# A token mixer with a chunked delta-rule recurrence: the recurrence's products as full 128x128 matmuls, k and r projected together

## The chip, the core and the metric

One core of a Trainium2 chip runs the whole step in one launch. Five engines work side by side, each through its own queue in order: TensorE (PE) multiplies matrices into PSUM, VectorE (DVE), ScalarE (ACT) and GpSimd (POOL) compute, SyncE (SP) issues transfers. The metric is the time of one execution on the device in microseconds, lower is better.

## What is computed

One layer on 2048 prompt tokens and on 8 sequences of 8 sample tokens, width 1024, all in float32. A convolution branch of 512 columns and a recurrent branch of 8 heads of 64 read the same normalised input, and an output projection joins them.

```python
xn = rms_norm(x, norm_g)
p = xn @ w_in                                # 1024 x 4224
# convolution branch: four groups of 512 columns
u = cg * h
z = conv_w[0]*u_ext[:, 0:T] + conv_w[1]*u_ext[:, 1:T+1] + conv_w[2]*u_ext[:, 2:T+2]
y_conv = bg * z * silu(gc)
# recurrent branch: r, k, v, two low-rank inputs (wl, al) and a gate, mixed with the previous token
pr = pr + mu_shift * (pr_prev - pr)
decay = exp(-DECAY_SCALE * sigmoid(w0 + tanh(wl) @ w_dec2))
a = sigmoid(a0 + al @ w_a2)
# per token and head, S is 64 x 64
sa = S @ (-kk_t)
S = S * w_t + sa (kk_t * a_t)^T + v_t k_t^T
o_t = S @ r_t
# group norm of o per head, bonus, gate; then
y = concat(y_conv, y_rwkv) @ w_out;  return rms_norm(x + y), states
```

## The kernel before, in words

Tokens stand along the free axis, features on the partitions. The prompt is done in two halves of 1024 tokens (`hf`), each in three blocks (`half_blocks`, line 79): 256, 384 and 384 tokens, in chunks of 64; the sample tokens ride with block 0 of the first half as one more chunk. The 8 heads are 4 pairs; one pair fills 128 partitions, head 0 above head 1. The main loop (line 915) makes 8 steps, one for each half and pair.

A projection (`project`, line 297) multiplies one or two tiles of 128 columns of `w_in` with a block: 24 matmuls for a tile and block, since inputs and weights are each split into a high and a low part of type float32r (three products, 8 slices of the 1024 rows). `load_w` (line 288) loads a tile's weights in two pieces and splits them on ACT and POOL; there are two buffers each for the high and the low part.

A step does, in program order:

- `rwkv_pair` (line 415). Tile k for all blocks, then tile r for all blocks, into two long tiles of the `hp` buffers (four of them); then v and the gate g in turn, and between them the front of each block. `after_k` makes the decays, their running products W, the scaled vectors `L` (first 64 columns from k, last 64 from r) and `bk`; `after_r` calls `amat`, which multiplies `bk` with `L` for each chunk and head, and masks the product into `AB` (solve matrix and output matrix) and into the other half of `L`; `store_blocks` sends the diagonal 32x32 blocks of `AB` out; `after_v` makes the bonus.
- `inverse` (line 625). Loads these blocks (`na`) and solves 32 columns by forward substitution on DVE (`subst`, two DVE instructions a row), sends the result round through DRAM into `AB`, and makes the off-diagonal blocks with 32x32 matmuls, with ACT and DVE reading one PSUM tile in turn (lines 671, 672).
- `wkv` (line 711), the recurrence. `group_tiles` transposes `bk` and v of up to four chunks. Then each `chunk` (line 714): L with state and v, the copy `xs`, AB with `xs`, the scaling `u` (line 736), `bt` with u, and the new state by two DVE instructions (line 740) that also read `tS`, the decayed old state (ACT). Each matmul is done once for each head, on 64 of the 128 rows or columns; an f32 matmul runs as two passes. Outputs add up in `oo`, one tile for a block, and `gn_out` normalises and stores them.
- `conv_group` (line 317), one of the four groups of the convolution branch: four single projections, h, C, B and G. At step 3 it comes before the next half's `xprep` and the inverse.

The framework orders the instructions when it builds: each engine takes what comes first in the program among what its own timing model has ready. So the projections of `conv_group` and of the next pair stand between the recurrence's matmuls in PE's queue. `T(pool, shape, tag, bufs)` is a tile out of `bufs` buffers. All waits are made by the framework; accesses of two engines to one PSUM tile are put in turn. PSUM has eight banks: `pj` 2 (projections), `ax` 2 (fronts), `cx` 1 (transposes, inverse), `ca`, `cb`, `oo` 1 each (recurrence).

The last part (`out_tile`, line 882) multiplies 17 tiles of up to 128 tokens with `w_out`, 48 matmuls of 512 columns each.

Of the kernel before, what the change touches and what calls it, by code (L numbers as in the profile page):

```python
# [10 lines left out]
BF16 = mybir.dt.bfloat16  # L11
# [25 lines left out]
C_MASK, C_SMASK, C_SCM, C_SCS, C_BM = 0, 128, 256, 640, 704  # L37
NMASK = 712
# [5 lines left out]
def constants():  # L44
# [11 lines left out]
    m[:, C_MASK:C_MASK + 64] = strict  # L56
    m[:, C_MASK + 64:C_MASK + 128] = incl
    m[:, C_SMASK:C_SMASK + 64] = strict & same
    m[:, C_SMASK + 64:C_SMASK + 128] = incl & same
# [28 lines left out]
def trunk_kernel(ctx, tc, I, O):  # L88
# [24 lines left out]
    def tmp():  # L113
        return T("tmp", [128, TW], "t", 7)
# [12 lines left out]

    def mm(out, lhsT, rhs, start=True, stop=True):
        pe.matmul(out, lhsT=lhsT, rhs=rhs, start=start, stop=stop)  # L129
# [3 lines left out]
    # constants and parameters  # L133
# [22 lines left out]
    def load_masks():  # L156
        for q in range(2):
            m = slice(q * NMASK // 2, (q + 1) * NMASK // 2)
            t = tmp()[:, :NMASK // 2]
            act.dma_start(out=t, in_=I["masks"][:, m])  # L160
            pool.tensor_copy(out=msk[:, m], in_=t)
# [26 lines left out]
    def rsqrt(x, n, rows=128, tag="x"):  # L188
        """x <- 1/sqrt(x) on [rows, n] of positive floats."""
# [14 lines left out]
    # normalised inputs, transposed and split  # L204
# [4 lines left out]
    def xprep(hf):  # L209
# [8 lines left out]
        def staging():  # L218
            stage[0] += 1
            if stage[0] % 6 == 5:  # L220
                return T("half", [128, HALF + SAMP], "la1", 1)[:, :D]
            if stage[0] % 6 == 0 and hf == 0:
                return T("pair", [128, 32, 32], "na", 1).rearrange("p a b -> p (a b)")
            return T("half", [128, 1108], "hp", 4)[:, :D]
# [63 lines left out]
    def load_w(src):  # L288
        wh = T("w", [128, KT, 128], "wh", 2, F32R)
        wl = T("w", [128, KT, 128], "wl", 2, F32R)  # L290
        for q in range(2):
# [24 lines left out]
    # convolution branch  # L316
    def conv_group(xs, hf, g):
        sp = 80 if hf == 0 else 0
        u = T("half", [128, 1108], "hp", 4)
        z = T("half", [128, 1108], "hp", 4)  # L320
        us = u[:, 0:80].rearrange("p (b j) -> p b j", j=10)
        up = u[:, sp:sp + 2 + HALF]

        def ev_h(bl, ps):
            if bl.samp:
                copy(us[:, :, 2:10], s9(ps)[:, :, 1:9])
                copy(us[:, :, 0:2], stc[:, g, :].rearrange("p (b j) -> p b j", j=2))
            if bl.i == 0:
                copy(up[:, 0:2], ucarry[:, g, :])
            copy(up[:, 2 + bl.p0:2 + bl.p0 + bl.np], ps[:, bl.c0:bl.cols])  # L330

        def ev_c(bl, ps):
            if bl.samp:
                mul(us[:, :, 2:10], us[:, :, 2:10], s9(ps)[:, :, 1:9])
                for b in range(1):
                    zs = s8(z)
                    copy(zs, us[:, :, 0:8], scale=pcol(P_CW, g))
                    stt(zs, us[:, :, 1:9], pcol(P_CW, 4 + g), zs, ALU.mult, ALU.add)
                    stt(zs, us[:, :, 2:10], pcol(P_CW, 8 + g), zs, ALU.mult, ALU.add)
# [3 lines left out]
            a, n = bl.p0, bl.np  # L343
            cur = up[:, 2 + a:2 + a + n]
            mul(cur, cur, ps[:, bl.c0:bl.cols])
            zp = z[:, bl.o:bl.o + n]
            copy(zp, up[:, a:a + n], scale=pcol(P_CW, g))
            for j in (1, 2):
                t = tmp()[:, 0:n]
                copy(t, up[:, a + j:a + j + n], scale=pcol(P_CW, 4 * j + g))  # L350
                pool.tensor_tensor(out=zp, in0=zp, in1=t, op=ALU.add)
            if bl.i == 2:
                copy(ucarry[:, g, :], up[:, HALF:HALF + 2])
                if hf == 1:
                    act.dma_start(out=O["conv_p"][:, g, :], in_=ucarry[:, g, :])
# [17 lines left out]

        yield from project(xs, hf, (g * 128, ev_h))
        yield from project(xs, hf, (2 * CW + g * 128, ev_c))
        yield from project(xs, hf, (CW + g * 128, ev_b))
        yield from project(xs, hf, (3 * CW + g * 128, ev_g))

    # token shift
    def shifter(hf, i, dst):  # L380
        state = {}

# [628 lines left out]
```

## Time and profile before

| | |
|---|---|
| median of 3 runs | 1671.4 us (1671.36 to 1675.69) |
| span of the profiled execution | 1669.8 us |
| instructions | 29362 |
| PE busy | 1548.2 us, 93% |
| DVE busy | 1046.6 us, 63% |
| ACT busy | 652.7 us, 39% |
| POOL busy | 338.2 us, 20% |
| projections and output, PE matmuls (`pj`) | 5568 |

Busy times come from one profiled execution. Matmuls are pipelined: one's time from start to end is longer than the distance to the next one's start, so the distance of starts tells what a matmul costs PE. The granted clock is 1.00 at full speed (2.4 GHz) and 0.5 at the lower level (1.2 GHz); the share given for a stretch is a mean.

### The profile page before, as it was taken

What the parts mean: (1) busy time and instruction counts of PE and PEld (TensorE: products, weight loads), DVE (VectorE), ACT (ScalarE), POOL (GpSimd) and SP (SyncE); (2) the same over time, 40 slices, a digit from 0 to 9 for tenths busy, and PEclk for the clock granted to TensorE, in tenths of its full rate; (3) what the DMA queues carried; (4) which work ended last, traced back from release to release, by engine and by line L of the source; (5) the groups of instructions that cost most, each with busy time, mean ns of one, the idle gap of its engine ahead of it and who ended that gap; (6) DMA issues with size and microseconds to landing.
All of it is one profiled execution on the core that took longest, in us unless ns stands there. A gap on an engine that the chain in (4) does not pass through costs nothing.

```text
span 1669.8 us, 29362 instructions
## 1 busy us (share of the span) xinstructions
PE 1548.2 (93%) x11088; PEld 1293.2 (77%) x11088; DVE 1046.6 (63%) x3101; ACT 652.7 (39%) x1657; POOL 338.2 (20%) x395
## 2 busy tenths in 40 slices
PE   4989999989989999879988998899989999899997
PEld 4979778887778778867778778877887788567885
DVE  6377557765776469775577457745774577566554
ACT  5333345324532455254442454245424542342221
POOL 3233112421032103321033112311231123100000
PEclk9989999899989999989989998999899989799999
DMA  5101201120012102331012101210121023523441
GB/s 170 50 28 44 62 30 31 44 67 29 21 47 56 47 23 60 92 96 37 22 34 63 46 23 35 63 46 23 34 63 46 23 59 92 155 77 124 139 145 51
DMA packets 112463, 99.99 MB, mean 60 GB/s; under 512 B 61561, under 2 KB 85625, under 8 KB 112322
## 3 DMA queue, kind: packets, MB, share of 16 engines
q1 hardware_dynamic: 107024, 87.23, 18.0%
q10 hardware_dynamic: 5266, 10.86, 1.8%
q8 instruction: 88, 1.44, 0.4%
q14 instruction: 53, 0.43, 0.1%
q0 software_dynamic: 32, 0.03, 0.0%
HBM read 75.30 MB, written 22.75 MB: 59 GB/s over the span
## 4 chain that ended last, share of the span: by engine, by line
PE 64%; DVE 22%; DMA 5%; issue 4%; ACT 3%; SPq 1%; POOL 1%; POOLq 0%; ACTq 0%; DVEq 0%
PE pj L129 42%; PE ca L129 5%; PE ax L129 5%; DVE sub L123 5%; DVE xi L123 4%; PE cb L129 4%; PE oo L129 2%; DVE hp L123 2%; PE cx L129 2%; DMA na<-dn 2%; DVE bk L123 1%; DVE t L120 1%; PE cx L688 1%; DVE hp L120 1%; PE ax L282 1%
## 5 line engine op out<-in xcount | busy, mean ns | idle before, releaser
L129 PE MATMUL pj<-xh,wh 128*128 128x384 f32 (+3 forms) x1856 | 660.5, 356 | 31.8 <-DVE hp L123 30.4
L129 PE MATMUL pj<-xh,wl 128*128 128x384 f32 (+3 forms) x1856 | 658.8, 355 | 0.0
L129 PE MATMUL pj<-xl,wh 128*128 128x384 f32 (+3 forms) x1856 | 656.3, 354 | 2.6 <-POOL xl L207 2.2
L129 PEld LDWEIGHTS pj<-xh,wh 128*128 128x128 f32 x1856 | 360.3, 194 | 69.4 <-DVE hp L123 28.3
L129 PEld LDWEIGHTS pj<-xl,wh 128*128 128x128 f32 x1856 | 361.1, 195 | 30.2 <-POOL xl L207 3.0
L129 PEld LDWEIGHTS pj<-xh,wl 128*128 128x128 f32 x1856 | 360.2, 194 | 27.2 <-issue 2.7
L207 POOL TENSOR_TENSOR wl<-wr,wh 128x512 fp32r<-128x512 f32 x132 | 173.4, 1328 | 459.0 <-ACT wh L117 321.4
L117 ACT ACTIVATE wh<-wr 128x512 fp32r<-128x512 f32 x132 | 80.2, 625 | 162.9 <-PE pj L129 119.1
L117 ACT ACTIVATE tS<-sv,wc 64x64 f32<-64x64 f32 x256 | 88.0, 344 | 130.2 <-DVE sv L120 104.3
L129 PE MATMUL ax<-L,bk 64*128 64x128 f32 x528 | 89.5, 325 | 35.7 <-DVE bk L123 25.8
L129 PEld LDWEIGHTS ax<-L,bk 64*128 64x128 f32 x528 | 74.0, 219 | 54.2 <-POOL wl L207 26.7
L120 DVE SCALAR_TENSOR_TENSOR sv<-cb,wc,tS 64x64 f32<-64x64 f32 x240 | 67.9, 283 | 63.5 <-PE cb L129 52.2
L123 DVE TENSOR_TENSOR sub<-xi,na 128x126 f32<-128x126 f32 (+22 forms) x248 | 91.1, 367 | 17.3 <-DMA na<-dn 10.0
L117 ACT ACTIVATE t<-pj,prm 128x384 f32<-128x384 f32 (+3 forms) x170 | 68.8, 433 | 62.7 <-PE pj L129 59.5
L516 POOL TENSOR_TENSOR bk<-t,t 64x384 f32<-64x384 f32 (+2 forms) x56 | 56.2, 1003 | 173.8 <-ACT t L488 91.4
L736 DVE TENSOR_SCALAR u<-ca,Q 128x64 f32<-128x64 f32 x128 | 36.2, 283 | 85.7 <-PE ca L129 85.4
L123 DVE TENSOR_TENSOR xi<-xi,sub 128x126 f32<-128x126 f32 (+22 forms) x248 | 83.0, 335 | 7.3
L129 PEld LDWEIGHTS ca<-sv,L 128*64 128x64 f32 x528 | 43.4, 136 | 38.6 <-DVE sv L120 12.2
L726 DVE COPY xs<-ca 128x64 f32<-128x64 f32 x128 | 28.7, 225 | 68.7 <-PE ca L129 58.5
L129 PE MATMUL ca<-sv,L 128*64 128x64 f32 x528 | 68.4, 247 | 0.0
L123 DVE TENSOR_TENSOR AB<-ax,msk 64x384 f32<-64x384 f32 (+2 forms) x88 | 48.6, 553 | 28.9 <-PE ax L129 27.9
L123 DVE TENSOR_TENSOR hp<-pj,hp 128x512 f32<-128x512 f32 (+1 forms) x34 | 23.4, 689 | 62.6 <-PE pj L129 61.7
(201 smaller groups left out, 2027.1 us busy)
## 6 DMA issues: line engine op xcount, KB each, us to landing
wr<-in_w_in SPq DMA_DIRECT2D x132, 256.0 KB, 2.7
hp<-in_x_prompt SPq DMA_DIRECT2D x29, 512.0 KB, 3.7
la<-yd SPq DMA_DIRECT2D x16, 512.0 KB, 3.9
out_y_p<-hp ACTq DMA_DIRECT2D x16, 512.0 KB, 2.7
na<-dn SPq DMA_DIRECT2D x16, 256.0 KB, 4.0
hp<-in_w_out SPq DMA_DIRECT2D x8, 512.0 KB, 4.1
yd<-hp SPq DMA_DIRECT2D x16, 192.0 KB, 1.9
yd<-c SPq DMA_DIRECT2D x16, 192.0 KB, 1.9
```

The costliest lines, as they stand in the source:

```text
L117: act.activation(out=out, in_=in_, func=AF.Copy, scale=scale, bias=bias)
L120: eng.scalar_tensor_tensor(out=out, in0=in0, scalar=scalar, in1=in1, op0=op0, op1=op1)
L123: dve.tensor_tensor(out=out, in0=in0, in1=in1, op=op)
L129: pe.matmul(out, lhsT=lhsT, rhs=rhs, start=start, stop=stop)
L207: eng.tensor_tensor(out=lo, in0=src, in1=hi.bitcast(F32), op=ALU.subtract)
L282: pe.transpose(out=ps[:, k, :], in_=xt[:, kk * 128:(kk + 1) * 128], identity=ident)
L516: pool.tensor_tensor(out=S.bk[bl.i][hs, chs, h, :], in0=ta[hs, a:a + n].rearrange("p (c j) -> p c j", j=64), in1=wi[hs, a:a + n].rearrange ...
L688: pe.transpose(out=pb[:, i, :], in_=S.bk[bi][:, ca + i].rearrange("p a t -> p (a t)"), identity=ident)
L726: dve.tensor_copy(out=xs_, in_=px)
L736: dve.tensor_scalar(out=u, in0=pu, scalar1=S.Q[:, q:q + 1], scalar2=None, op0=ALU.mult)
```

## The change

The recurrence: `bk` is transposed in the front, block by block, into `G` (one 128x128 block for each head and chunk, made of the transposed `bk` in the head's columns and the masked output matrix in the other head's columns). A chunk is then two products of L for 128 columns, one product of both heads' solve (`AB` of this and the next chunk as 128 columns, times a block-diagonal `xd`), and two products of G, which give the state's part and the output's part at once. Outputs are read once for each group of up to four chunks, by an ACT copy and a DVE sum. The first copy and the scaling are each divided between DVE and ACT by heads; `tS` moves to POOL. `L`, `G`, `AB` are made once and kept; `bk` has two buffers for three tiles.

The projections: k and r are projected together, block by block, into tiles of one block (`kr`, three buffers), and `after_kr` runs the block's front right behind them; v with g, h with C and B with G likewise. Weights are loaded in three pieces. The buffers `hp` go from four to two and `t` from seven to four, with tiles of their own for `sq`, `td`, `ta`. The matmuls of `amat` alternate between the heads. The bonus product with v moves to POOL.

```diff
     def load_w(src):
...
-        for q in range(2):
-            wr = T("w", [128, 4, 128], "wr", 2)
-            sync.dma_start(out=wr, in_=src[:, q * 4:q * 4 + 4, :])
-            split(wh[:, q * 4:q * 4 + 4, :], wl[:, q * 4:q * 4 + 4, :], wr, pool)
+        for k in (slice(0, 3), slice(3, 6), slice(6, 8)):
+            raw = T("w", [128, 3, 128], "wr", 2)[:, :k.stop - k.start, :]
+            sync.dma_start(out=raw, in_=src[:, k, :])
+            split(wh[:, k, :], wl[:, k, :], raw, pool)
...
+    LP, GP, ABP = [[], []], [[], []], []
+    for i, mx in enumerate((5, 6, 6)):
+        for h in range(2):
+            LP[h].append(T("pair", [128, mx, 128], f"L{h}{i}"))
+            GP[h].append(T("pair", [128, mx, 128], f"G{h}{i}"))
+        ABP.append(T("pair", [128, mx + 1, 64], f"AB{i}"))
+    XD = [T("pair", [128, 128], f"xd{i}") for i in range(2)]
...
         def amat(bl, ca, n, smask=False):
...
+            pas = [AX([128, n, 128]) for h in range(2)]
+            for i in range(n):
+                for h, hs in heads():
+                    mm(pas[h][:, i, :], bk[hs, ca + i].rearrange("p a t -> p (a t)"), L[h][hs, ca + i, :])
...
             for h, hs in heads():
...
+                mul(AB[hs, cs, :], pas[h][hs, :, hs], m(hs, 0, 64))
+            ab = AB[:, cs, :]
             pool.tensor_tensor(out=ab, in0=ab, in1=S.Q[:, q0:q0 + n].unsqueeze(2).to_broadcast([128, n, 64]), op=ALU.mult)
...
+            pb = CX([128, n, 128])
+            for i in range(n):
+                pe.transpose(out=pb[:, i, :], in_=bk[:, ca + i].rearrange("p a t -> p (a t)"), identity=ident)
+            for h, hs in heads():
+                copy(G[h][:, cs, hs], pb[:, :, hs])
+            for h, hs in heads():
+                mul(L[h][other(h), cs, :], pas[h][other(h)], m(other(h), 64 * h, 128))
+                mul(G[h][hs, cs, other(h)], pas[h][hs, :, other(h)], m(hs, 64, 64))
...
+        yield from project(xs, hf, (CONV_COLS + CW + p * 128, shifter(hf, 4 + p, to_tmp("k"))),
+                           (CONV_COLS + p * 128, shifter(hf, p, to_tmp("r", after_kr))))
+        yield from project(xs, hf, (CONV_COLS + 2 * CW + p * 128,
+                                    shifter(hf, 8 + p, lambda bl: (S.v[bl.i], lambda: after_v(bl)))),
+                           (CONV_COLS + 3 * CW + 128 + p * 128, shifter(hf, 13 + p, to_tmp("g", after_g))))
...
     def chain_banks():
-        return PS([128, 4, 64], "ca", 1), PS([128, 2, 64], "cb", 1)
+        return [PS([128, 2, 4, 64], f"ch{h}", 1) for h in range(2)] + [PS([128, 4, 128], "cu", 1)]
...
             for h, hs in heads():
-                mm(px[hs], L[h][:, c, 0:64], sv[:, i, h, :])
+                mm(pc[h][:, 0, i, :], S.L[h][bi][:, c, :], sv[:, i, h, :])
+            xd = XD[i % 2]
+            if sample is None:
+                tS = T("ch", [128, 64], "tS", 2)
+                for h, hs in heads():
+                    pool.tensor_scalar(out=tS[hs], in0=sv[hs, i, h, :], scalar1=S.wc[hs, wc:wc + 1], scalar2=None,
+                                       op0=ALU.mult)
+                dve.tensor_copy(out=xd[0:64, 0:64], in_=pc[0][0:64, 0, i, :])
+                copy(xd[64:128, 64:128], pc[1][64:128, 0, i, :])
...
+            pu = pc[2][:, i, :]
+            mm(pu, S.AB[bi][:, c:c + 2, :].rearrange("p c t -> p (c t)"), xd)
+            dve.tensor_scalar(out=sv[0:64, i, 0, :], in0=pu[0:64, 0:64], scalar1=S.Q[0:64, q:q + 1], scalar2=None,
+                              op0=ALU.mult)
+            copy(sv[64:128, i, 1, :], pu[0:64, 64:128], scale=S.Q[64:128, q:q + 1])
             for h, hs in heads():
+                mm(pc[h][:, 1, i, :], S.G[h][bi][:, c, :], sv[:, i, h, :])
...
                 for h, hs in heads():
+                    stt(nxt(h)[hs], pc[h][hs, 1, i, :], S.wc[hs, wc:wc + 1], tS[hs], ALU.mult, ALU.add)
...
+            for h, hs in heads():
+                os_ = other(h)
+                o_ = ob[os_, ca:ca + n, :]
+                copy(o_, pc[h][os_, 0, 0:n, :])
+                tt(o_, pc[h][os_, 1, 0:n, :], o_, ALU.add)
```

## Rows read from the trace of the kernel before

**Rows 1.** The page, part 1: busy us, share of span, instructions.

```profile
PE 1548.2 (93%) x11088; PEld 1293.2 (77%) x11088; DVE 1046.6 (63%) x3101; ACT 652.7 (39%) x1657; POOL 338.2 (20%) x395
```

**Rows 2.** The page, part 4: the chain that ended last, by engine.

```profile
PE 64%; DVE 22%; DMA 5%; issue 4%; ACT 3%; SPq 1%; POOL 1%; POOLq 0%; ACTq 0%; DVEq 0%
```

**Rows 3.** Windows: us, busy (instructions) of PE, PEld, DVE, ACT, POOL; PEclk, DMA, GB/s.

```profile
1216.00:1250.00 34.00, 29.76 (x169) 28.95 (x168) 24.88 (x70) 7.36 (x15) 10.92 (x10) 0.90 0.19 56
1250.00:1268.00 18.00, 18.00 (x219) 16.25 (x218) 6.61 (x15) 5.91 (x18) 4.35 (x6) 1.00 0.37 88
1268.00:1330.00 62.00, 62.00 (x562) 45.82 (x562) 30.37 (x125) 28.65 (x86) 5.59 (x6) 1.00 0.07 24
1330.00:1383.00 53.00, 48.77 (x274) 43.77 (x274) 42.37 (x99) 24.36 (x56) 17.05 (x18) 0.87 0.20 56
```

**Rows 4.** Timeline of PE, one chunk: start, us to the last end, what, xcount.

```profile
1301.02 0.34 PE L129 MATMUL pj<-xh,wh 128*128 128x384 f32 x1
1301.29 0.33 PE L129 MATMUL cb<-u,bt 64*64 64x64 f32 x4
...
1301.67 0.45 PE L129 MATMUL pj<-xl,wh 128*128 128x384 f32 x1
1301.95 0.34 PE L129 MATMUL pj<-xh,wl 128*128 128x384 f32 x1
1302.22 0.33 PE L129 MATMUL ca<-sv,L 128*64 128x64 f32 x2
...
1303.03 0.44 PE L129 MATMUL pj<-xh,wh 128*128 128x384 f32 x1
1303.31 0.34 PE L129 MATMUL pj<-xl,wh 128*128 128x384 f32 x1
1303.58 0.33 PE L129 MATMUL ca<-xs,AB 64*64 64x64 f32 x4
1303.84 0.44 PE L129 MATMUL pj<-xh,wl 128*128 128x384 f32 x1
1304.12 0.34 PE L129 MATMUL pj<-xh,wh 128*128 128x384 f32 x1
1304.29 0.33 PE L129 MATMUL pj<-xl,wh 128*128 128x384 f32 x1
```

**Rows 5.** Timeline of PE around six full f32 passes in a front.

```profile
311.20 0.34 PE L129 MATMUL pj<-xl,wh 128*128 128x384 f32 x1
311.38 0.72 PE L129 MATMUL ax<-cst,t 128*128 128x2 f32 x6
311.96 0.42 PE L129 MATMUL pj<-xh,wl 128*128 128x384 f32 x1
312.22 0.34 PE L129 MATMUL pj<-xh,wh 128*128 128x384 f32 x1
```

**Rows 6.** Groups by line: busy us, mean ns of one | idle before <-releasers.

```profile
L129 PE MATMUL ax<-L,bk 64*128 64x128 f32 x528 | 89.5, 325 | 35.7 <-DVE bk L123 25.8 <-DVE nwyg L120 4.0 <-DVE L L123 3.1
L736 DVE TENSOR_SCALAR u<-ca,Q 128x64 f32<-128x64 f32 x128 | 36.2, 283 | 85.7 <-PE ca L129 85.4
L672 DVE COPY na<-cx 32x192 f32<-32x192 f32 (+1 forms) x24 | 8.2, 341 | 20.1 <-ACT na L117 19.8
L117 ACT ACTIVATE tS<-sv,wc 64x64 f32<-64x64 f32 x256 | 88.0, 344 | 130.2 <-DVE sv L120 104.3 <-DVE nwyg L196 8.4 <-DVE gv L841 7.5
L760 POOL COPY sv<-sst 64x64 f32<-64x64 f32 x16 | 3.8, 236 | 32.6 <-PE cb L129 32.1
L207 POOL TENSOR_TENSOR wl<-wr,wh 128x512 fp32r<-128x512 f32 x132 | 173.4, 1328 | 459.0 <-ACT wh L117 321.4 <-PE pj L129 126.5 <-DMA AB<-dx 6.7
L194 DVE TENSOR_SCALAR nwag<-gv 128x6 int32<-128x6 int32 (+2 forms) x24 | 5.6, 235 | 0.4
```

**Rows 7.** Timeline of DVE while POOL multiplies bk.

```profile
1334.31 0.71 DVE L194 TENSOR_SCALAR nwag<-gv 128x6 int32<-128x6 int32 x1
```

**Rows 8.** The page, part 6: DMA issues, KB each, us to landing.

```profile
hp<-in_x_prompt SPq DMA_DIRECT2D x29, 512.0 KB, 3.7
```

More of the change, by code (lines that the diff above doesn't have):

```diff
@@ L126, in mul, with heads, other @@
         tt(out, in0, in1, ALU.mult)
+    def heads():
+        return ((0, slice(0, 64)), (1, slice(64, 128)))
+    def other(h):
+        return slice(64 - 64 * h, 128 - 64 * h)
     def mm(out, lhsT, rhs, start=True, stop=True):
@@ L406, in shifter, with clear_blocks @@
         return ev
+    LP, GP, ABP = [[], []], [[], []], []
[5 more added lines that the diff above has]
+    XD = [T("pair", [128, 128], f"xd{i}") for i in range(2)]
+    def clear_blocks():
+        for i in range(3):
+            pool.memset(ABP[i], 0.0)
+            for h, hs in heads():
+                pool.memset(GP[h][i][other(h), :, other(h)], 0.0)
+        for t in XD:
+            pool.memset(t, 0.0)
     class Pair:
@@ L468, in after_k @@
             decays(bl)
[L469 to L470 removed]
+            sq, td, ta = (T("tmp", [128, TW], n, 1) for n in ("sq", "td", "ta"))
+            cc, cum = sq, td
+            act.activation(out=sq[:, :nt], in_=kb, func=AF.Square, scale=pcol(P_KK, p))
+            pq = AX([128, 4, 2])
+            for j in range(bl.nch // 2):
+                a = (SAMP if bl.samp else 0) + j * 128
+                mm(pq[:, j, :], sq[:, a:a + 128], hsel)
+            if bl.samp:
+                mm(pq[0:64, 3, :], sq[:, 0:64], hsel)
             act.activation(out=td[:, :nt], in_=pd, func=AF.Tanh, scale=0.5, bias=hwa[:, p:p + 1])
@@ L682, in group_tiles @@
     def group_tiles(S, bi, ca, n):
-        bt = T("ch", [128, 4, 128], "bt", 2)
         sv = T("ch", [128, 4, 2, 64], "sv", 2)
-        pb = CX([128, 4, 128])
-        for i in range(n):
-            pe.transpose(out=pb[:, i, :], in_=S.bk[bi][:, ca + i].rearrange("p a t -> p (a t)"), identity=ident)
-        copy(bt[:, 0:n, :], pb[:, 0:n, :])
         o = ca * 64
@@ L722, in chunk @@
             if sample is None:
                 for h, hs in heads():
-                    vs = slice(64, 128) if h == 0 else slice(0, 64)
-                    mm(pm[hs], bt[vs, i, hs], sv[vs, i, h, :], start=True, stop=False)
-                dve.tensor_copy(out=xs_, in_=px)
-                tS = T("ch", [128, 64], "tS", 2)
-                for h, hs in heads():
-                    copy(tS[hs], sv[hs, i, h, :], scale=S.wc[hs, wc:wc + 1])
-            else:
-                tt(xs_, px, sample, ALU.add)
@@ L747, in chunk @@
-            for h, hs in heads():
-                mm(po[hs], AB[hs, c, 64:128], us[h][hs], start=False, stop=True)
+                    stt(nxt(h)[hs], pc[h][hs, 1, i, :], S.wc[hs, wc:wc + 1], tS[hs], ALU.mult, ALU.add)
         groups = []
@@ L801, in sample_chunk @@
         for a in range(2):
-            copy(pts[:, a, :].rearrange("p (b j) -> p b j", j=8), pp_[:, :, a, :])
+            for h, hs in heads():
+                copy(pts[hs, a, :].rearrange("p (b j) -> p b j", j=8), pp_[hs, :, a ^ h, :])
         pt = CX([128, 128])
@@ L805, in sample_chunk @@
         xo = T("ch", [128, 8, 64], "c2", 4)[:, :2]
-        for a in range(2):
-            for h, hs in heads():
-                copy(xo[hs, a, :], pt[a * 64:a * 64 + 64, hs])
-        po = PS([128, 1, 64], "oo", 1)
-        chunk(0, 0, 0, None, bt, sv, 0, po[:, 0], None, chain_banks(), sample=xo[:, 0, :])
-        tt(ob[:, 0, :], po[:, 0], xo[:, 1, :], ALU.add)
+        for h, hs in heads():
+            copy(xo[hs, 0, :], pt[0:64, hs])
+            copy(xo[other(h), 1, :], pt[64:128, hs])
+        pc = chain_banks()
+        chunk(0, 0, 0, None, sv, 0, None, pc, sample=xo[:, 0, :])
+        for h, hs in heads():
+            os_ = other(h)
+            tt(xo[os_, 1, :], pc[h][os_, 0, 0, :], xo[os_, 1, :], ALU.add)
+            tt(ob[os_, 0, :], pc[h][os_, 1, 0, :], xo[os_, 1, :], ALU.add)
         zm = T("ch", [128, 8, 64], "c2", 4)[:, :8]
```

243 lines of the change are left out of this document (93 added, 150 removed).

## The prediction, made before the change was run

> **What bounds the kernel now.** I read the busy shares first [rows 1]: TensorE (PE) is busy 93% of 1669.8 us, VectorE 63%. The reader is to see that only PE comes near the span; the chain that ended last says the same, PE 64% and DVE 22% of it [rows 2]. The time outside the profiled span is the median less the span, 1.6 us (0.1%); I add nothing for it and work against 1669.8.
>
> An average hides four stretches, so next I cut one period of the second half (167 us, one head pair) into windows [rows 3]. 1216 to 1250: the substitution on DVE, PE filled by the convolution's projections, clock 0.90. 1250 to 1268: the rest of the inverse. 1268 to 1330: the recurrence, 16 chunks in 62 us, 3.87 us each; PE is busy every microsecond at full clock, DVE 30 of 62. 1330 to 1383: the next pair's front (decays, L, bk, the masked products): DVE 42 of 53, PE's clock 0.87. So the recurrence is bound by PE, the front by DVE and its hand-overs, and they stand one behind the other.
>
> What PE does in a chunk is in its timeline [rows 4]. From 1301.02 to 1304.29 is one chunk, 3.27 us. Two projection matmuls side by side start 0.17 apart (1304.12, 1304.29); seven of them start in the chunk, 1.19 us. The other **2.08 us** are three groups of small matmuls, 24 passes (an f32 matmul is two). It is not the passes that cost: four 64x64 passes end within 0.33 us, but from the last projection matmul before such a group to it are 0.27 us where 0.17 is usual (1303.31 to 1303.58), and the first one after it keeps the next away 0.28 (1303.84 to 1304.12). Entering and leaving a small group costs about 0.1 each.
>
> **The change, part by part.**
>
> *Chunk on PE.* 24 small passes become 10 full ones: 4 with L, 2 with the pair of AB blocks, 4 with G. The nearest full f32 passes are the six with 2 columns [rows 5]: between 311.20 and 312.22 lie two projection matmuls (0.34) and six passes, so 0.68 us, 0.113 a pass, entering and leaving included. Ten are 1.13. Saved: 0.95 x 132 chunks (the front's 528 passes of L with bk are four a chunk [rows 6]) = **-125 us** of PE. Bounds: 0.08 a pass (four 64x64 passes in 0.33 [rows 4]) gives -169; if enter and leave stay at 0.2 for each of three groups, the saving is 0.35, -46. I take the six full passes; they are the same kind with the same weights' width.
>
> Here a page speaks against the change. The Trainium skill (TensorEngine Tiling (Array Packing), Theoretical Speedup) promises up to 2x where one dimension is at most 64, by cutting the array into tiles, which this edit gives up; the same page (Key Properties) says that changing the tiling mode drains the array. The 0.1 on either side of a group agrees with the second. By the first alone the saving would be nil (rival 4).
>
> *Front on PE.* The 528 passes of L with bk (mean 325 ns [rows 6]) stay, but alternate between the heads' row halves and fill two banks at once. Between 0 and half of their 89.5 us; DVE sets this stretch, so I take -10. Transposes of bk move from the chunk groups into the front, same number; their copies become two for each group instead of one, on ACT.
>
> *Chain of a chunk.* The hand-overs stay five (L, copy, AB, scale, G, update), but three things change. The scale was one DVE instruction, 283 ns [rows 6]; now DVE scales one head and ACT the other out of one PSUM bank. The program makes them take turns: where before both read one bank (line 672) DVE sat 19.8 us over 24 times for ACT [rows 6]. One 64x64 ACT step is 344 ns: +0.34 a chunk. At the end of each group of up to four chunks ACT copies and DVE adds the outputs before the next group may write those banks: two steps of at least 0.28 and 0.34 with hand-overs, about 0.9, five groups a pair, +0.28 a chunk. tS goes from ACT to POOL, beside the matmuls: 236 ns for a 64x64 copy [rows 6], nothing on the path unless POOL's queue is in a weight split of 1.33 us [rows 6]. Shorter PE groups give back 0 to 0.95; I take 0.3.
>
> POOL beside DVE has a price that a row shows: a 6-element DVE step takes 0.71 us while POOL multiplies bk [rows 7]; its mean is 0.24 [rows 6]. The Trainium skill (SBUF — State Buffer, Who interferes with whom) lets a DVE step with one SBUF input outside the two-port modes run free of POOL. If it holds for the chain, whose steps read PSUM, this price is nil; the row is the other bound.
>
> *Front in time.* k and r now come block by block, into three small tiles, with the block's front right behind, and L, G, AB are held per block. Block 0 of the next pair can write its L once the recurrence has passed block 0. So two of three block fronts can lie inside the recurrence, where DVE is idle half the time; only block 2 must follow it: 53 becomes 18 (bounds 18 and 53). Its DVE steps queue with the chain: between 0 and (0.71 - 0.24) x 5 = 2.4 a chunk; I take +0.5, one such wait.
>
> Recurrence: 3.87 + 0.34 + 0.28 - 0.30 + 0.50 = 4.69 a chunk, 75 us. Period: 34 + 18 + 75 + 18 = 145 for 167, -22.
>
> *Weights.* All projections now run in pairs, so both weight buffers are taken until the pair ends; before, single tiles let the next load ahead. A tile's split is 2 x 1.33 us of POOL [rows 6], three pieces instead of two, the same elements. It lies under 24 matmuls of the first tile's block 0, 4.1 us at 384 columns and 2.7 at 256 (by columns). Cover is just short, 0.5 us x 32 pairs: **+15** (0 to 43, one uncovered piece each).
>
> *At nothing:* conv's u per block, the split L copies, bonus product on POOL, clearing the blocks at the start (POOL waits for loads there). Staging and output tiles have 2 buffers for 4: a 512 KB load is 3.7 us [rows 8], an output tile is 48 matmuls of 512 columns, about 11 us, so it stays covered; uncovered, 17 x 3.7 = +63.
>
> **Two sums.** By PE work: 1669.8 - 125 - 10 + 15 = 1550, all of today's idle time and slow clock kept. By stretches: six periods with a successor in the same half, 6 x -22 = -132; the last pair runs beside the output projection, where PE is the bound, 17 x -0.95 = -16; +15: 1537. I forecast **1540**.
>
> **Rivals.**
> 1. *PE alone.* If the fronts overlap so well that PE never waits, more comes back: per period it is idle 8.5 us and loses 0.10 x 34 + 0.13 x 53 = 10 us to the clock [rows 3]. Half of these 18.8 over eight pairs is 75, all of it 150: 1550 - 75 = 1475, or 1400; I put it at 1450. For: DVE is at 63%. Against: the substitution stays, and PE has only the convolution beside it.
> 2. *The chain takes it.* The 0.2 around a group belongs to waiting for its operand, not to the small tile, and stays: 1669.8 - 46 - 10 + 15 = 1629. Or POOL's hold on DVE adds 1 us a chunk, 16 us x 6: 1636. Against the first: the six full passes entered without it. For the second: [rows 7].
> 3. *Slower: the front stays outside.* k1, r1 need the small tiles that block 0's front releases, v and g need the weight buffers of k and r, and the front needs the one transposing PSUM bank that the recurrence uses too. If so all three fronts follow the recurrence, and the recurrence is longer: 34 + 18 + 75 + 53 = 180, +13 x 6 - 16 + 15 = **1747**. It decides at 40 us of front outside (167 - 34 - 18 - 75): one block must get in. Against: block 0 needs only its own L, and DVE is free half of the recurrence.
> 4. *Nothing gained*: the small tiles' side-by-side passes were worth as much as their gaps cost, so that a full pass takes 2.08 / 10 = 0.21, and the stretches stay where they are: 1669.8 - 10 + 15 = 1675. Against: 0.113 in [rows 5]. It is what the tiling page's speedup would make of it.
>
> **How the numbers follow.** Forecast 1490 to 1590: 0.54. Rival 1: 0.15. Rival 2 (1590 to 1660): 0.17. Rival 3: 0.11. Rival 4: 0.03, as "same". A measurement of this kernel tells about 0.3% (5 us) from no change. Faster 0.54 + 0.15 + 0.17 = 0.86, same 0.03, slower 0.11. The range goes from 1435 (rival 1 less its lower half) to 1650 (rival 2 less its end), leaving out about 0.05 below and 0.15 above.
>
> **What would show it.** Right: a chunk's small matmuls take near 1.1 us of PE, without the 0.27 and 0.28; in the recurrence L and bk steps of the next pair stand between the chain's steps on DVE; the front behind it is some 18 us. A chunk lasts over 4 us with less PE in it. Wrong: full passes far from 0.113 (the first term), a front still of 50 us (rival 3), chunks over 5.5 us (rival 2), or PE idle at the first blocks of paired projections for more than 0.5 us each.

## The result, and the profile after

The changed kernel takes **1725.8 us** (median of 4 runs, 1723.3 to 1729.4) where the kernel before takes 1672.8 beside it: ratio **1.031** (95% interval 1.026 to 1.036), slower. The forecast was 1540, range 1435 to 1650.

The page of the changed kernel, parts 1 and 2 (the last line is the granted clock in tenths over 40 slices), and the span with its mean granted clock. Set them beside [rows 1]:

```profile
span 1724.3 us, 27152 instructions
PE 1534.7 (89%) x9272; PEld 1333.8 (77%) x9272; DVE 1045.1 (61%) x3257; ACT 703.0 (41%) x2004; POOL 500.4 (29%) x753
PEclk8969998989989989868677996989899999998999
core 0: 1724.3 us, clock 0.900
```

1816 fewer matmuls, but only 13 us less of busy PE. The clock tells why: its mean falls from 0.950 to 0.900, and the low slices stand together around the 20th of 40. Idle time (span less busy) rises from 122 to 190 us. So each span is split three ways below: PE's work as it would be at full clock (busy time, less half of what lies in stretches at 1.2 GHz), what the slow clock adds, and idle time. That halving is a working assumption; it is near what the passes of L with `bk` show in the kernel before, which start 0.112 us apart at full clock and 0.213 at 1.2 GHz (medians). The three columns add up to the span.

| kernel | span | work at full clock | added by the slow clock | idle |
|---|---|---|---|---|
| before | 1669.8 | 1472.5 | 75.7 | 121.6 |
| after | 1724.3 | 1394.0 | 140.7 | 189.6 |

The change took 78 us of work from PE and lost 65 to the clock and 68 to idle time. The loss is in two places. From the end of pair 2's recurrence to the end of pair 3's, the passage between the two halves, are 197 us before (626 to 823) and 287 after (617 to 904), 90 more. The part behind the last recurrence is 36 us longer, and all the rest is 71 shorter. Windows of the changed kernel in the passage (columns as in [rows 3]): the rest of the convolution at step 3; the gap; the solve of pair 3; its recurrence:

```profile
652.00:716.00 64.00, 61.04 (x358) 59.51 (x356) 11.02 (x26) 20.12 (x55) 21.23 (x25) 1.00 0.22 63
716.00:753.00 37.00, 16.10 (x68) 13.38 (x69) 18.80 (x41) 15.11 (x30) 5.49 (x7) 0.55 0.30 99
753.00:808.00 55.00, 40.53 (x326) 36.73 (x325) 37.07 (x110) 24.16 (x63) 12.45 (x14) 0.81 0.16 42
808.00:901.00 93.00, 80.94 (x398) 67.28 (x397) 53.09 (x191) 37.60 (x120) 22.02 (x43) 0.70 0.06 17
```

The same place in the kernel before, also from the end of pair 3's front: convolution and solve side by side, the second half's input, the recurrence:

```profile
673.00:713.00 40.00, 35.55 (x208) 34.28 (x207) 30.21 (x91) 11.83 (x26) 11.14 (x11) 1.00 0.30 87
713.00:750.00 37.00, 26.01 (x250) 21.19 (x247) 27.21 (x66) 22.48 (x49) 9.83 (x9) 0.82 0.37 104
750.00:821.00 71.00, 71.00 (x638) 52.13 (x637) 36.82 (x139) 35.42 (x104) 8.81 (x9) 1.00 0.11 34
```

PE works 16 of 37 us from 716, the clock drops to a mean of 0.55, and the recurrence then runs at 0.70. In the changed kernel the solve, which before ran beside the convolution (DVE 30 of 40 us), has moved behind the second half's input. Timelines of the changed kernel, SP, ACT, POOL and DVE in turn (start, us, engine, line, operation; in brackets idle time before it and what ended it):

```profile
656.45 1.14 SPq L649 DMA_DIRECT2D na<-dn  x2
...
737.67 1.06 ACT L252 ACTIVATE c<-hp 128x1024 bf16<-128x1024 f32 x1 [1.88 <-DMA hp<-in_x_prompt]
...
742.71 2.35 POOL L266 TENSOR_TENSOR hp<-hp,la 128x1024 f32<-128x1024 f32 x1 [22.52 <-ACT hp L116]
745.00 0.52 POOL L644 MEMSET c<- 128x512 f32 x1
...
752.69 0.69 DVE L212 TENSOR_TENSOR xl<-ax,xh 128x512 fp32r<-128x512 f32 x1 [0.83 <-ACT xh L116]
753.29 0.18 DVE L122 TENSOR_TENSOR sub<-c,na 128x31 f32<-128x31 f32 x1
```

The solve's blocks `na` are loaded from 656.45. Its first step is at 753.29. In between its result tile was not to be had: the change has moved it,

```diff
-        x = T("pair", [128, 16, 32], "xi", 1)
+        x = T("ch", [128, 16, 32], "c2", 4)
```

and `c2` is also the ring (the buffers of one tag, taken in turn; here four) into which `xprep` writes the thrown-away squares of the eight input tiles of the second half, which come first in the program. The fifth of these eight squares must be done before x gets its buffer; each square waits for its input (the fifth, at 737.67, 1.88 us for the load), and the inputs come through few `hp` buffers (the first square ran at 676, the second at 724). The clearing of x (745.00) then stands behind POOL's work on the input, and the first step behind DVE's. The line isn't in the excerpt of the diff above, and the words there don't name it. The kernel before starts the same step at 688.42:

```profile
688.42 0.18 DVE L123 TENSOR_TENSOR sub<-xi,na 128x31 f32<-128x31 f32 x1
```

One period of the second half, from the end of one recurrence to the end of the next, before (167 us) and after (159 us):

```profile
1163.00:1330.00 167.00, 158.47 (x1215) 134.79 (x1214) 104.17 (x309) 65.96 (x174) 38.15 (x42) 0.94 0.15 41
```

```profile
1220.00:1379.00 159.00, 148.69 (x998) 132.73 (x997) 104.23 (x328) 71.81 (x215) 58.48 (x86) 0.94 0.16 43
```

PE has 9.8 us less to do, the period is 8 us shorter, the clock the same. Here the change works, at a third of the 22 us that were forecast. Three periods of the second half take 165, 150 and 159 us for 173, 167 and 167 before, so the gain lies between 8 and 17.

### The profile page after: what moved, and what is told of

It reads as the page before. It is cut to its first block, busy times and chain, and to the rows that moved or that the text cites. A ratio compares the mean times of both kernels' runs of the same rounds, so it can differ in the third digit from the quotient of the medians.

```text
span 1724.3 us, 27152 instructions
## 1 busy us (share of the span) xinstructions
PE 1534.7 (89%) x9272; PEld 1333.8 (77%) x9272; DVE 1045.1 (61%) x3257; ACT 703.0 (41%) x2004; POOL 500.4 (29%) x753
## 4 chain that ended last, share of the span: by engine, by line
PE 56%; DVE 23%; DMA 6%; ACT 5%; issue 5%; POOL 3%; SPq 1%; POOLq 0%; DVEq 0%; ACTq 0%
PE pj L134 35%; PE ax L134 8%; PE ch L134 6%; DVE sub L122 4%; DVE c L122 4%; PE cu L134 2%; DMA wr<-in_w_in 2%; PE cx L134 2%; POOL wl L212 1%; DVE c L119 1%; DMA hp<-in_x_prompt 1%; DVE bk L122 1%; DMA dx<-c 1%; SPq L678 1%; ACT sv L116 1%
## 5 line engine op out<-in xcount | busy, mean ns | idle before, releaser
L212 POOL TENSOR_TENSOR wl<-wr,wh 128x384 fp32r<-128x384 f32 (+1 forms) x198 | 185.4, 947 | 287.4 <-ACT wh L116 260.2
L732 POOL TENSOR_SCALAR tS<-sv,wc 64x64 f32<-64x64 f32 x256 | 124.7, 487 | 309.5 <-DVE sv L119 222.9
L116 ACT ACTIVATE wh<-wr 128x384 fp32r<-128x384 f32 (+1 forms) x198 | 93.9, 483 | 123.4 <-DMA wr<-in_w_in 70.1
L134 PEld LDWEIGHTS ch<-sv,G 128*128 128x128 f32 x528 | 87.5, 202 | 37.3 <-DVE sv L741 24.7
L134 PE MATMUL ch<-sv,G 128*128 128x64 f32 x528 | 104.7, 286 | 10.9 <-DVE sv L741 8.2
L119 DVE SCALAR_TENSOR_TENSOR sv<-ch,wc,tS 64x64 f32<-64x64 f32 x240 | 67.8, 283 | 62.6 <-PE ch L134 54.3
L134 PEld LDWEIGHTS ch<-sv,L 128*128 128x128 f32 x528 | 91.3, 202 | 15.6 <-DVE c L122 3.2
L134 PE MATMUL ch<-sv,L 128*128 128x64 f32 x528 | 100.4, 280 | 3.0 <-DVE c L122 0.9
L122 DVE TENSOR_TENSOR sub<-c,na 128x126 f32<-128x126 f32 (+22 forms) x248 | 88.2, 356 | 13.6 <-DMA na<-dn 6.5
L122 DVE TENSOR_TENSOR c<-c,sub 128x126 f32<-128x126 f32 (+22 forms) x248 | 80.9, 326 | 7.9
## 6 DMA issues: line engine op xcount, KB each, us to landing
wr<-in_w_in SPq DMA_DIRECT2D x66, 128.0 KB, 2.2
```

Source lines behind the costliest of these rows:

```text
L116: act.activation(out=out, in_=in_, func=AF.Copy, scale=scale, bias=bias)
L119: eng.scalar_tensor_tensor(out=out, in0=in0, scalar=scalar, in1=in1, op0=op0, op1=op1)
L122: dve.tensor_tensor(out=out, in0=in0, in1=in1, op=op)
L212: eng.tensor_tensor(out=lo, in0=src, in1=hi.bitcast(F32), op=ALU.subtract)
L732: pool.tensor_scalar(out=tS[hs], in0=sv[hs, i, h, :], scalar1=S.wc[hs, wc:wc + 1], scalar2=None, op0=ALU.mult)
```

## The experiments

All ratios are to the kernel before, with their 95% intervals; the changed kernel's is 1.031.

**Theory A**: the shared ring `c2` holds the solve of pair 3 back. **Theory B**: the staging and output tiles, two buffers for four, do.

**a1_solve_own.** The solve's tile alone, put into a ring whose next buffer is free then:

```diff
-        x = T("ch", [128, 16, 32], "c2", 4)
+        x = T("pair", [128, 6, 2, 64], "bk", 2).rearrange("p a b c -> p (a b c)")[:, :512]
+        x = x.rearrange("p (c t) -> p c t", t=32)
```

> The changed kernel, with the solve's tile x taken from the bk ring (its second buffer, idle at that time) instead of the c2 ring that the squares of the second half's input also go through. Theory A (the shared ring): the solve of pair 3 no longer waits for the second half's input; it runs at about 655 to 690 us instead of 753 to 791, the recurrence of pair 3 begins before 740 instead of at 808, TensorE does not fall to half clock for most of 716 to 935, and the total falls by 60 to 90 us, to 1635 to 1665. Theory B (only two staging buffers hp): the input still arrives late, the solve's place changes nothing in what ends last, total 1705 to 1725.

Measured 1679.3, 1.003 (1.001 to 1.006): 46 us of 53 are back with one tile. Its DVE timeline:

```profile
661.89 0.18 DVE L122 TENSOR_TENSOR sub<-bk,na 128x31 f32<-128x31 f32 x1
```

The solve is 91 us earlier. The gain is below the 60 to 90 expected: pair 3's recurrence began at 732 us and then stood until 771. ACT's and PE's timelines of a1:

```profile
758.87 1.06 ACT L252 ACTIVATE c<-hp 128x1024 bf16<-128x1024 f32 x1 [1.23 <-DMA hp<-in_x_prompt]
758.88 0.34 ACTq L794 DMA_DIRECT2D c<-in_state_wkv  x1
...
761.68 0.99 PE L134 MATMUL cx<-L,c 64*64 64x16 f32 x28 [1.11 <-DMA c<-in_state_wkv]
```

The sample chunk of pair 3 loads its state into `c2` too, and the load could go only when the last square had been started (758.87).

**b1_ring_in_before.** The same line the other way round: the kernel before with x in `c2`.

> The kernel before with one part of the change alone: the solve's tile x in the c2 ring. Theory A: its solve of pair 3 falls behind the second half's input as well, the recurrence of pair 3 begins 30 us or more later than at 750, and the total rises by 25 to 70 us: 1698 to 1743. Theory B: the kernel before has four staging buffers, its input comes in time, the total rises by under 10 us.

Measured 1719.4, 1.026 (1.022 to 1.030), 44 us slower than before. Its solve starts at

```profile
731.18 0.18 DVE L123 TENSOR_TENSOR sub<-c,na 128x31 f32<-128x31 f32 x1
```

for 688.42. The ring alone makes the kernel before nearly as slow as the changed one.

**a4_junk_own.** The changed kernel with the squares' result in another ring, x in `c2`:

```diff
-                    junk = T("ch", [128, KT, 128], "c2", 4, BF16)
+                    junk = T("pair", [128, 12, 128], "bk", 2, BF16)[:, :KT]
```

> The changed kernel, with the thrown-away result of the squares of the second half's input written to the bk ring, so that neither the solve's tile nor the five tiles of pair 3's sample chunk in the c2 ring wait behind that input. In a1_solve_own (1679) the solve came early, but its recurrence stood from 732 to 780 us, since the sample chunk's state tile still waited in c2 for the last square at 758.8. Theory A (the ring is the whole coupling): the recurrence of pair 3 runs on from about 730 with no gap, total 20 to 40 us below a1: 1640 to 1660. Theory B (what ends last there is the input's own arrival through two buffers): the recurrence moves, the front of pair 4 starts no earlier, total 1668 to 1682.

Measured 1665.6, 0.995 (0.993 to 0.997). 60 us of the changed kernel's time were this ring: by a1, b1 and a4 theory A holds for the sign. But a4 lies between its two ranges, 14 us below a1 where theory A wanted 20 to 40: the recurrence of pair 3 begins at 746, not 730, and takes 100 us. So the ring is not shown to be the whole coupling.

**a2_tail_buffers, a7_wout_staging, a10_x_tiles.** Theory B in the tail. a2 takes tiles for `w_out` and for the output's x in turn from four places:

```diff
+    def tail():
+        turn[0] += 1
+        if turn[0] % 4 == 2:
+            return [(T("pair", [128, 32, 32], "na", 1).rearrange("p a b -> p (a b)"), slice(0, D))]
+        if turn[0] % 4 == 0:
+            return [(T("pair", [128, 6, 2, 64], "bk", 2).rearrange("p a b c -> p (a b c)")[:, :512],
+                     slice(q * 512, q * 512 + 512)) for q in range(2)]
+        return [(T("half", [128, 1108], "hp", 2)[:, :D], slice(0, D))]
```

> The changed kernel, with four buffers instead of two in turn for the staging of w_out and for the x tiles of the output (two hp, the solve's na, and two halves in the bk ring); nothing else. Theory B: the eight w_out tiles arrive within 30 us instead of 50, more output tiles run beside the last recurrence, the end after it is 15 to 35 us shorter: total 1690 to 1710. Theory A alone: the tail is TensorE's own work and moves by under 8 us: 1717 to 1726.

Measured 1710.0, 1.022 (1.018 to 1.025), 16 us less. Windows from the end of the last recurrence to the end, in the changed kernel and in a2:

```profile
1533.00:1724.00 191.00, 169.39 (x725) 134.36 (x724) 97.06 (x312) 39.55 (x90) 0.00 (x0) 0.95 0.36 121
```

```profile
1540.00:1708.00 168.00, 159.01 (x691) 126.19 (x691) 94.07 (x313) 38.88 (x89) 0.00 (x0) 0.98 0.39 129
```

Then each half of a2 alone. a7, `w_out` alone:

> The changed kernel with half of a2: four buffers in turn for the staging of w_out alone, the output's x tiles in the two hp buffers as in the change. After the last projection of the changed kernel TensorE is idle 17.6 us, in a2 2.1. Theory S (w_out's rows come through one free buffer, since the convolution's z holds the other): a2's whole gain of 16 us is here, 1705 to 1714. Theory X (the x tiles of the output): under 5 us, 1719 to 1726.

Measured 1725.9, 1.030 (1.024 to 1.037): it gains nothing, so theory S fell. a10, the x tiles alone:

> The changed kernel with the other half of a2: four buffers in turn for the output's x tiles alone, w_out's staging in the two hp buffers. a7_wout_staging showed that staging alone gives nothing. Theory X (the x tiles): all of a2's gain, 1703 to 1715, TensorE idle under 5 us after the last projection. If it takes both halves: 1719 to 1728.

Measured 1716.2, 1.022 (1.017 to 1.028). That is a2's ratio, though the time is just above theory X's range and the interval reaches far: the x tiles, most likely.

**b3_tail_two.** The kernel before with two tiles, made once and used in turn, for `w_out` and x.

> The kernel before with the tail alone restricted as the change does: w_out's staging and the output's x tiles go through two buffers in turn instead of four. Theory B (the buffers of the tail): 15 to 35 us slower, 1688 to 1710. Rival: the tail is TensorE's own work, and the 35 us that the changed kernel lost there are output tiles that its shorter recurrence could not hold: under 6 us, 1668 to 1680.

Measured 1674.3, 1.001 (0.999 to 1.003). Theory B's price doesn't show there, and the rival's range was met; two buffers of their own are enough. In the changed kernel the same two also hold the convolution's `z`; that this is the difference was not tried.

**a3_both.** a1 and a2 together.

> Both: the solve's tile in the bk ring and four buffers in the tail. If A and B each hold for its own stretch, the gains add, 80 to 115 us off 1726: 1610 to 1645, faster than before (1673). If one is only a shift of the other's loss, the sum is no better than the better of the two alone. If the packed recurrence and the paired projections gained nothing beside these two, no better than 1665.

Measured 1657.6, 0.989 (0.985 to 0.993): faster than before. The two gains add (46 and 16; together 71), but the expected 1645 wasn't reached, as a1 had fallen short.

**a5_no_staging, a6_all_buffers.** a5 is a4 with a2. a6 also puts the solve of pair 3 ahead of the second half's input in the program, and so frees `na` to be a staging buffer for that input, four in turn:

```diff
-            run(conv_group(xs, hf, p))
-            xs = xprep(1)
-        run(inverse(S))
+            run(conv_group(xs, hf, p))
+        run(inverse(S))
+        if s == 3:
+            xs = xprep(1)
```

> The changed kernel with all three: the squares' result in the bk ring; the solve of pair 3 put ahead of the second half's input in the program, so that na is free to be a staging buffer of that input (four in turn: hp, la1, hp, na); and four buffers in the tail as in a2. If the couplings are what the change lost, 1600 to 1640. If only the ring and the tail matter and staging does not, as a4 less about 20 us. If it is no better than a3_both (1658), neither the sample chunk's wait nor the staging was on the path.

> a6_all_buffers without its third part: the squares' result in the bk ring and four buffers in the tail, but the second half's input through hp, hp and la1 as in the change, and ahead of the solve in the program. a4 (1666) and the tail's gain (16) make 1650. If the staging is worth nothing, 1620 to 1632 as a6; if two staging buffers for four hold the second half back, 1642 to 1657.

a5 1642.6, 0.978 (0.972 to 0.984); a6 **1626.0, 0.972** (0.968 to 0.975). Order and staging together have some 10 to 17 us (the intervals overlap); which of the two it is was not tried. a6 has the lowest median of all runs, 2.8% faster than before, and does the whole change's arithmetic. What it doesn't give back is pair 3's recurrence, 97 us for 73 before. Its span and clock, and that recurrence:

```profile
core 0: 1627.8 us, clock 0.937
```

```profile
744.00:841.00 97.00, 85.68 (x547) 72.29 (x546) 77.03 (x238) 63.42 (x176) 35.72 (x53) 0.91 0.12 37
```

**b2_front_by_block.** From here on the question is what the parts of the change are worth. The kernel before with the front's order alone:

```diff
+        yield from project(xs, hf, (CONV_COLS + CW + p * 128, shifter(hf, 4 + p, to(k))),
+                           (CONV_COLS + p * 128, shifter(hf, p, to(rr, after_kr))))
```

> The kernel before with another part of the change alone: k and r projected together block by block, the k and r work after each block's r, v and g after all of k and r; the recurrence, the buffers and the weights as before. The forecast took 22 us per pair from the change, with the front's work brought into the recurrence (53 to 18 us of it outside). Theory F (where the front lies is worth something by itself): 4 to 10 us less per pair, 1595 to 1645. Theory P (TensorE's work is the bound of a pair: it is busy 159 of 167 us wherever the front lies): within 15 us of before, 1660 to 1690.

Measured 1645.0, 0.983 (0.980 to 0.987). 29 us, 3.6 a pair: theory F in sign, just short of its 4.

**b4_weights_three.** The kernel before with weights in three pieces.

> The kernel before with the weights alone brought in as in the change, three pieces for two, the same elements. The forecast took +15 (0 to 43) for the paired weights. If the number of pieces costs, 1680 to 1700; if POOL and the queue hold them easily, within 4 us of before. This leaves the pairing out: b2_front_by_block pairs k with r and was faster.

Measured 1641.9, 0.980 (0.975 to 0.985), 36 us faster; no theory had that.

**c3_order_and_weights.** b2 and b4 together.

> The kernel before with the two parts of the change that were each faster alone: front block by block (b2, 29 us) and weights in three pieces (b4, 35 us); the recurrence is not packed. If they take different waits away, the gains add: 1600 to 1620. If both shorten the same wait of TensorE at the front, 1630 to 1645. Set beside c1 or c2 it tells what packing the recurrence is worth with the buffers mended: by TensorE's work at full clock (1472 before, 1394 after) up to 78 us; if c1 and c2 come out no lower than this run, nothing.

Measured 1642.1, 0.981 (0.976 to 0.986): no gain over either. **c4_weights_two** undoes the three pieces in the mended packed kernel (c1, below):

> c1_scratch_in_place (1630) with the weights brought in two pieces as before the change (the memory for it comes from c1's scratch). In the changed kernel TensorE's projections wait 9.2 us for ACT's half of a split and 8.3 for POOL's. If the three pieces were what gained 35 us in b4: 1645 to 1665 here. If the number of pieces changes no wait that matters and b4's gain came with the order of work that the planner chose (c3, with the same edit, gained nothing over b2): within 8 us, 1622 to 1638. If three pieces cost what TensorE waits for: 1608 to 1620.

Its ratio is 0.991 (0.988 to 0.995) for c1's 0.972 (0.968 to 0.977): three pieces gain there. So they help in two of three kernels. How they do it stays open.

**b5_front_temporaries.** b2 with the front's temporaries as in the change (the squares come earlier in the front for it, as there).

> The kernel of b2_front_by_block (1645) with the front's temporaries as in the change: one tile each for the square, the decay and the gate, reused within a block, and four instead of seven shared ones. The first recurrence begins at 166 us in b2 and at 184 in the changed kernel. Theory T (single temporaries hold one block's front behind the one before): the first recurrence begins 6 us or more later than in b2 and the total rises by 10 to 30 us, 1655 to 1675. Rival (the 18 us are the masks, the transposes in the front and the clearing): within 6 us of b2, 1639 to 1651.

Measured 1694.5, 1.010 (1.004 to 1.017), by the ratios 45 us above b2. But the first recurrence begins 3 us later only (169 for 166), so theory T had the sign, but neither the size (10 to 30) nor the place. In its trace the whole difference to b2 is the clock's part (table below). **c1_scratch_in_place** and **c2_shared_seven** then took those temporaries out of a6:

> The kernel of a6_all_buffers (1626) with the front's three single temporaries put where they need no memory of their own and where each block has its own: the square and the decay in the block's L tile of the second head, the gate in the block's AB tile, both written anew later in the same front. Theory T (single temporaries hold the blocks of the front behind one another, +49 in b5 against b2): 20 to 50 us faster, 1575 to 1606. Rival (in the packed kernel another tile, the bk ring or the k and r tiles, holds the blocks anyway): within 8 us of a6, 1618 to 1634.

> c1 with the memory that it frees given to the shared temporaries, seven in turn as before the change instead of four. If b5's loss came from the shared four as much as from the single three, another 8 us or more below c1; if from the single three alone, within 6 us of c1.

Measured 1629.6, 0.972 (0.968 to 0.977), and 1630.6, 0.975 (0.971 to 0.980): no change from a6. Theory T fell for the packed kernel, and b5's loss isn't explained. b4 and b5 together say that an edit can move this kernel by 36 or 45 us without a wait that anyone had named; a total alone is weak evidence here. For the ring the timelines show the wait itself come and go.

**a8_one_engine.** a6 with both heads' scales and copies on DVE.

> The kernel of a6_all_buffers (1626) with one edit in the chunk: both heads' scales of u and both copies into xd on VectorE, none on ScalarE. Theory H (the heads drift apart on two engines, so TensorE enters more small groups, each with its price): a little fewer groups, 4 to 15 us faster, 1610 to 1622. Rival (a chunk's steps on VectorE are the chain): two more steps of 0.28 us a chunk, 8 x 16 x 0.56 = 72 us of VectorE, of which a third or more shows, 1640 to 1665. If neither: within 4 us.

Measured 1644.9, 0.982 (0.977 to 0.987): 18 us slower than a6, in the rival's range, though a quarter of its 72 and not a third. The chunk is better divided between two engines, as the change has it.

The split of the span for these kernels, as above:

| kernel | span | work at full clock | added by the slow clock | idle |
|---|---|---|---|---|
| b1 | 1718.1 | 1462.4 | 127.7 | 128.0 |
| b2 | 1639.3 | 1465.8 | 55.0 | 118.5 |
| b4 | 1641.2 | 1477.7 | 48.1 | 115.4 |
| b5 | 1702.6 | 1454.2 | 122.2 | 126.2 |
| c3 | 1639.7 | 1470.0 | 56.1 | 113.6 |
| a1 | 1672.3 | 1395.9 | 107.6 | 168.8 |
| a6 | 1627.8 | 1394.5 | 91.4 | 141.9 |

All kernels of one recurrence have the same work, within 24 us; what tells them apart is the clock, and in the packed ones idle time. Packing takes about 75 us of work off PE, and a6's span keeps 12 of it against c3: 35 go to the clock and 28 to idle time. By the ratios a6 is 16 us below c3, c1 15 and c2 10; the intervals of c1 and c2 overlap c3's, and the two kernels differ in more than packing. So a gain of 10 to 16 us at most is shown for it.

## Why the prediction was wrong, point by point

*What bounds the kernel.* Right for the periods: PE is busy 148.7 of 159 us. It doesn't hold for the passage between the halves, which the prediction never looked at; its windows were all from the second half.

*At nothing: the step that gave the wrong sign.* The move of the solve's tile into `c2` wasn't on the list at all. It is one line of the diff, and costs 44 to 60 us (b1, a1, a4). The two buffers for four were on the list as covered, with 63 us if not: with the new order of a6 they make 39 (a4 to a6). Ring, buffers and order are the 99 us between the changed kernel and a6. "Covered" was worked out for a transfer by itself, 3.7 us [rows 8] under 11 us of matmuls. What they cost lay elsewhere. For `c2` the runs show where: who else is in the ring, and in which order they come. For the tail b3 shows only that the number two alone is not the cost.

*Chunk on PE: -125.* Right in kind, mis-sized: the 1.13 us of a chunk is 1.5, and the term about -85. All of PE's work fell by 78 us, front and weights included. A chunk of the changed kernel, PE's timeline, to be set beside [rows 4]:

```profile
1353.77 0.34 PE L134 MATMUL pj<-xh,wl 128*128 128x384 f32 x1
1353.95 0.33 PE L134 MATMUL ch<-sv,L 128*128 128x64 f32 x2
1354.09 0.42 PE L134 MATMUL pj<-xh,wh 128*128 128x384 f32 x1
1354.46 0.43 PE L134 MATMUL ch<-sv,L 128*128 128x64 f32 x2
1354.71 0.42 PE L134 MATMUL pj<-xl,wh 128*128 128x384 f32 x1
1354.96 0.34 PE L134 MATMUL pj<-xh,wl 128*128 128x384 f32 x1
...
1355.75 0.46 PE L134 MATMUL cu<-xd,AB 128*128 128x128 f32 x2 [0.28 <-ACT L L116]
1355.97 0.42 PE L134 MATMUL pj<-xl,wh 128*128 128x384 f32 x1
...
1356.65 0.43 PE L134 MATMUL ch<-sv,G 128*128 128x64 f32 x2
1356.90 0.42 PE L134 MATMUL pj<-xl,wh 128*128 128x384 f32 x1
1357.16 0.33 PE L134 MATMUL ch<-sv,G 128*128 128x64 f32 x2
1357.30 0.42 PE L134 MATMUL pj<-xh,wl 128*128 128x384 f32 x1
1357.56 0.33 PE L134 MATMUL pj<-xh,wh 128*128 128x384 f32 x1
```

The passes are cheap: two take 0.14 (1353.95 to 1354.09). But a price of entering and leaving a group stayed with full tiles, which the forecast held to be in the 0.113 of a pass: the projection matmul behind one keeps the next 0.25 away (1354.71 to 1354.96) where 0.17 is usual. And there are more groups, since the two heads now become ready one after the other, by DVE and by ACT: five in this chunk for three in [rows 4], and by the starts in the traces 576 for all 132 chunks (616 in a6) for 459. Counted from all starts of a recurrence at full clock (1269 to 1330 before, 1310 to 1377 after), a chunk's small matmuls cost PE 2.16 us before, near the 2.08 of the forecast, and 1.51 after: the passes fell from 1.57 to 0.95, entering and leaving only from 0.59 to 0.56. A group's own price fell from some 0.2 to 0.13, so a part of it doesn't belong to small tiles. Rival 2 said that the price of a group stays; its 46 was too low, 125 too high.

*Front on PE: -10.* Nothing came of it. At full clock a pass of L with `bk` starts 0.112 us behind the one before, in both kernels. The mean is 358 ns where [rows 6] has 325, but that is the clock: 215 of the 528 passes lie at 1.2 GHz, at least in part, for 136 before. Groups of the changed kernel (busy us, mean ns, idle before and its releasers):

```profile
L732 POOL TENSOR_SCALAR tS<-sv,wc 64x64 f32<-64x64 f32 x256 | 124.7, 487 | 309.5 <-DVE sv L119 222.9 <-DVE nwyg L201 21.1 <-DVE nwyg L119 14.3
L134 PE MATMUL ax<-L,bk 64*128 64x128 f32 x528 | 102.5, 358 | 6.4 <-POOL bk L525 3.9 <-ACT bv L116 1.6 <-DVE bk L122 0.6
L116 ACT ACTIVATE sv<-cu,Q 64x64 f32<-64x64 f32 x132 | 40.3, 305 | 80.2 <-DVE sv L741 53.9 <-DVE gv L119 6.8 <-DVE nwag L122 6.7
L741 DVE TENSOR_SCALAR sv<-cu,Q 64x64 f32<-64x64 f32 x132 | 36.3, 275 | 66.4 <-PE cu L134 63.9 <-POOL wl L212 0.6 <-POOL tS L732 0.5
```

*Chain of a chunk: 4.69 us.* It was 4.3 (69 us for 16, windows below). The turns of DVE and ACT on one bank came as forecast (ACT waits 53.9 us for DVE, 0.41 a chunk). `tS` on POOL takes 487 ns for 236, and DVE's update waits 3.4 us in all for it. The 0.5 a chunk for POOL's hold on DVE came as 0.14: POOL is busy 28 of 69 us in the recurrence, and four steps of the group norm are 2.2 us longer there than usual, but the scaling takes 275 ns where `u` took 283 [rows 6]. The Trainium skill (SBUF — State Buffer, Who interferes with whom) says that a VectorE step with at most one SBUF input, outside the two-port modes, doesn't contend with GpSimd; for the scaling, which reads PSUM, the row agrees.

*Front in time: 53 to 18.* Half right. Windows of a period after, as in [rows 3] but with the front first: front, substitution, rest of the inverse, recurrence:

```profile
1220.00:1258.00 38.00, 33.68 (x179) 28.82 (x178) 27.93 (x74) 16.17 (x46) 13.05 (x19) 0.82 0.13 37
1258.00:1288.00 30.00, 28.51 (x177) 28.01 (x177) 21.79 (x65) 9.04 (x27) 7.98 (x9) 1.00 0.21 57
1288.00:1310.00 22.00, 20.13 (x217) 17.53 (x215) 5.67 (x16) 7.76 (x22) 9.43 (x10) 0.84 0.30 62
1310.00:1379.00 69.00, 66.37 (x431) 58.37 (x431) 48.84 (x174) 38.84 (x122) 28.03 (x48) 1.00 0.11 35
```

The front outside the recurrence is 38 here and 34 in the next period, not 18: block 0 got in, blocks 1 and 2 did not; why block 1 did not stays open. 38 is under rival 3's point of 40, so its slower period did not come; that the total lies near its 1747 is chance.

*Period: -22.* -8 in the period shown, -17 and -8 in the two before it; in a6 the three take 151, 151 and 159 us for 173, 167 and 167 before. In the period shown the front gives back 15 us and the recurrence takes 7 of them; the other two windows change by 4 either way. PE has only 9.8 us less to do, so the stretches could not shrink by more without taking its idle time, and that stayed at 8 to 10 us a period.

*Weights: +15.* The three pieces alone have the other sign in b4 and c4 and do nothing in c3. What pairing alone costs was not measured.

*What is left.* From a6 to the sum by PE work, 1550, are 78 us: 57 of work not saved (78 for 135), 16 of clock and 20 of idle time that "all of today's idle time and slow clock kept" had left out, less the 15 for the weights. That a6 lies inside the stated range doesn't make the sum right.

## What to carry to other kernels

Go through a diff by rings: for each tile that joins a ring, list who else is in it, in program order, and what the one ahead waits for; one line that saved 2 KB (of each partition's memory) cost about as much as the whole change gains without it, 48 us in a6. Cut a period into windows, but also the passages that occur once. And a saving on the busiest engine counts only as far as its clock and its idle time stay; here 75 us of work became 12 us of time.

## What was not expected of the hardware

The slow clock lasts beyond the gap where it fell. In the changed kernel PE had 61 of 64 us busy at 1.00, then 16 of 37 at a mean of 0.55; over the recurrence behind it, with PE busy 81 of 93 us, the clock was 0.70. In b1 PE is busy 80 of 84 us in the same recurrence, at 0.72, where the kernel before has 71 of 71 at 1.00:

```profile
786.00:870.00 84.00, 80.23 (x590) 56.26 (x591) 45.17 (x158) 37.49 (x108) 5.35 (x10) 0.72 0.05 16
```

The clock isn't all that makes this recurrence long, though: in a6 it takes 97 us at a mean of 0.91, with DVE busy 77 of them, where DVE was busy 37 of 71 before. What holds it there stays open. Over whole kernels with the same work the clock's part goes from 48 us (b4) to 128 (b1).
